# A third split of one inner product in five stages of a three-level Strassen kernel, with an operand half made earlier and a later place for additions

## The chip, the cores and the metric

The kernel runs on one core of a Trainium2 chip. The metric is the device time of one execution in microseconds (us). The kernel before takes 1354.5 us (median of 3 runs, 1354.32 to 1354.63).

## The reference

```python
probs = softmax(router_logits, axis=-1)               # 16 x 512 x 8
for e in range(8):
    expert_out = np.matmul(x, expert_weights[e])      # x: 16 x 512 x 512, weights: 512 x 2048
    output += probs[:, :, e:e+1] * expert_out         # output: 16 x 512 x 2048, float32
```

Read as one product, 8192 rows of z (the row of x times each of the eight probabilities, 4096 values) are multiplied with a 4096 x 2048 matrix.

## The kernel before, in words

**Three levels.** The product is taken apart by the Strassen-Winograd scheme. At the outer level there are seven products P1 to P7 (the dictionary key `r` in `products[r, q]`), each for 16 row pairs `q`; one operand of a product is 256 rows (`HQ`) by 1024 columns of z as two tiles `t[0]` and `t[1]` of 128 x 8 x 256 (f16), the other a set of weight tiles. At the inner level each product is again seven *steps*, in the order 1, 5, 6, 2, 7, 3, 4 (`STEPS`); a step is 8 matmuls of 128x128 by 128x512 into one PSUM bank of 512 f32 columns. The step's letter a or b below says which of a stage's two products it belongs to (5a is step 5 of the first). At the third level, where it is used, one step of *both* products of a stage (16 matmuls of 512 columns) is replaced by seven *small* products of 4 matmuls of 256 columns each. They are called small 1 to small 7 here.

**Stages.** `add` makes a list of stages, each of one or two products, and `run(stage)` writes out its instructions. The order is P1 (7 stages), P2 (8), P5 and P6 together (17), then P7 and P4 in turn (16: a P7 stage of two products, then the P4 stage of the same rows), then P3 (9). `k5`, `k7` and `k3` are the first stages of P5/P6, of P7/P4 and of P3. `hooks[(stage, slot)]`, filled with `at`, holds loads and sums that are begun before a given slot (step) of a stage.

**Where the third level is used before.** `by_thirds` splits steps 1 and 5 in most stages (all P4 stages from the second on among them), `by_twos` step 2 in four P1 stages. P7's stages have none. In `by_thirds` the small products go through banks x and q; small 1 is copied by ScalarE (ACT) to the left half of bank g, small 2 is added on it by TensorE (PE), and small 3's result is added by VectorE (DVE) into the right half of g. Bank h gets small 7 in its right half (DVE) and small 4 in its left half (ACT, line L931). In `by_thirds` small 2 comes before small 3.

**Order of the work.** PE, DMA and the vector work all keep the order in which they are written. For DVE that order comes from a planner: `later` queues a task with a cost in us, and `slack`, called after each step, moves a clock for PE forward by the slot's length and issues tasks while the clock for DVE is behind it:

```python
def slack(slot=SLOT, lag=LAG):
    clock["dve"] = max(clock["dve"], clock["pe"])
    clock["pe"] += slot
    while queue and clock["dve"] < clock["pe"] - lag:
        queue.popleft().run()
```

After it comes the step's `post`: the addition or copy that takes the step's result out of its bank. Where a product has a base (P6, P7, P4), `post` of steps 1, 5, 6, 7, 3 and 4 is a DVE addition of 128x512 f32 with a tile of 128 x 512 f32 (`half()`, from a pool `h` of 12 tiles), and `post(1)` writes a further bank b on which step 2 accumulates. `need(task)` flushes the queue to a task whose result a step reads.

**Tiles of P7 and P4.** The eight tiles of a P7 stage's results serve as the base of the P4 stage behind it, and are freed when that stage's transfers to the output (POOL's queue, `out_dram<-h`) have landed. The next P7 stage's eight bases are fetched into h tiles in between (SP's queue, `h<-out_dram`), at slots 7, 9, 12 and 16 of the P4 stage, counted on into the P7 stage. `Left.make(k)` makes an operand half with one multiplication and one subtraction, `queue_s2` and `queue_i` make the sums `s2` (pool d, 3 tiles) and `i` from it; `queue_halves` queues them for the next P7 stage in the P4 stage, half 0 at slot 5 and half 1 at slot 11. `Thirds.queue` queues a P4 stage's operands in the P7 stage ahead of it.

**P3.** `turnover_in_place` loads P3's weights during the last P7/P4 pair and makes their sums: tasks of 2.29 us, put at the head of the queue. `EARLY` lists operand halves of P3 that are made during P6 and kept in DRAM.

Of the kernel before, what the change touches and what calls it, by code (L numbers as in the profile page):

```python
# [31 lines left out]
def kernel(  # L32
# [7 lines left out]
    nc = tc.nc  # L40
    P = 128
# [13 lines left out]
    HQ = 256  # L55
# [17 lines left out]

    def x_tile():
        return xpool.tile([P, C, HQ], f16, name="xs", tag="x")

    def h_tile(shape, dtype):
        return hpool.tile(shape, dtype, name="h", tag="h")
# [276 lines left out]
    SLOT = 1.73  # L355
    STEPS = (1, 5, 6, 2, 7, 3, 4)
    HP = HQ // 2
    LAG = 0.3
# [89 lines left out]
    class Left:  # L448
# [34 lines left out]

        def queue_s2(self):
            def make():
                self.s2 = spool.tile([P, K8, HP], f16, name="d", tag="d")
# [50 lines left out]
        def half(self, k):  # L537
            return self.t[k]

    class HalfLoadedLeft(Left):  # L540


        def __init__(self, xb, pb, kept, source):
            super().__init__(xb, pb, kept=kept)
            self.source = source

        def load(self):
            self.t[0] = new_z()
            sp(self.t[0], self.source)

        def queue_make(self, k):
            if k == 0:
                self.task[0] = None
            else:
                super().queue_make(k)

# [13 lines left out]
    class Thirds:  # L570
# [14 lines left out]
            tt(o, *(self.s[v] if isinstance(v, int) else v for v in (x, y)), op)  # L585
            self.s[p] = o

        def queue(self):
            self.a.queue_make(0)
            self.b.queue_make(0)  # L590
            for p in (5, 6, 3, 7):
# [3 lines left out]
            for left in (self.a, self.b):  # L595
                left.queue_make(1)

        def op(self, p, part):
            need(self.task[7])
            a, b = self.a.t[0], self.b.t[0]  # L600
            z = {1: a[:, 0:C], 2: a[:, C:K8], 4: b[:, C:K8]}.get(p)
            return (self.s[p] if z is None else z)[:, :, ds(part * HP, HP)]

    class Right:

# [45 lines left out]
    class Product:  # L651
# [4 lines left out]
            self.loads, self.banks, self.o = [], {}, {}  # L656
            self.apart = self.two = False

        def step(self, p):
            b = "q" if p in (5, 3) else "b" if p == 2 else "x"  # L660
            if p in (1, 5):
                self.banks[b] = (bank if p == 1 else bank2)()
# [100 lines left out]
    def left_of(r, q, fresh=True):  # L763
        a, b = 2 * q, 2 * q + 1
        if r == 1:
            pt = PBlock(a, P1, xp1[q - 2][1] if q in (2, 3) else None)
            if q in (2, 3):
                xs[a] = XBlock(a, xp1[q - 2][0])
            return Left(xblock(a), pt), [xblock(a), pt]
        if r == 2:  # L770
            pt = PBlock(a, P2)
            return Left(xblock(a), pt), [xblock(a), pt]
        if r == 7:
            pt = PBlock(b, P2)
# [11 lines left out]
        if r == 3 and q in EARLY:  # L786
            pa = PBlock(a, P2)
            return HalfLoadedLeft(xblock(a), pa, ZHalf(q, z_places[q]), operand3[q]), [xblock(a), pa]
# [44 lines left out]
        return p  # L833

    products = {}
    EARLY = {5: (5, 3), 8: (8, 3), 10: (10, 9)}
    operand3 = {q: dram.tile([P, K8, HQ], f16, name=f"operand3_{q}") for q in EARLY}
    z_room = []

    def z_place(i):  # L840
        def place():
            if i != 2:
                z_room.append(new_w().rearrange("p k (two t) -> p (k two) t", two=2))
            return z_room[-1][:, ds(i // 2 * K8, K8), :]
        return place
    z_places = {q: z_place(i) for i, q in enumerate((5, 8, 10))}


    def start_loads(stage):
# [90 lines left out]
    def by_twos(stage):  # L940
# [36 lines left out]

        def full(i, p):
            some[i].step(p)
            slack()  # L980
            some[i].post(p)
        for slot, todo in enumerate((((1,), (0, 6)), ((5,), (6,)), ((1, 6),), ((2,), (7,), (3,)), ((0, 7),), ((4,), (1, 7))), 4):
            for make in hooks.get((stage, slot), ()):
# [6 lines left out]
                finish_loads(stage + 2)  # L990
        return 10

    def queue_lefts(stage):
        if stage in thirds:
            if not thirds[stage].task:
                thirds[stage].queue()
        elif stage < len(stages):
            for p in stages[stage]:
                queue_left(p.left)

    def run(stage):
        some = stages[stage]
        if stage in twos:
            twos[stage].queue()
        for p in some:
            p.left.queue_i()
        n = by_thirds(stage) if stage in thirds else 0
        if stage in twos:
            n = by_twos(stage)
        for i in range(n // 2, len(some[0].steps)):  # L1010
            for p in some:
                for make in hooks.get((stage, n), ()):
                    make()
                p.step(p.steps[i])
                slack()
# [36 lines left out]
        add(product(4, q), product(4, q + 1))  # L1052
    xs.clear()
    k3 = add(product(3, 5))
    for q in ((8, 10), (0, 14), (1, 2), (3, 4), (6, 7), (9, 11), (12, 13)):
        add(*(product(3, i) for i in q))
    end = add(product(3, 15))
    for stage in range(k7, k3, 2):
# [18 lines left out]
            at(*where, lambda q=q, tn=tn: joined(q, tn))  # L1077
    at(k6 - 1, 8, lambda: queue_left(lefts[7, 14]))

    def queue_halves(q, k):  # L1080
        for i in range(2):
            lefts[7, q + i].queue_make(k)
        if k == 0:
            for i in range(2):
                lefts[7, q + i].queue_s2()
    for n, q in enumerate(ORDER_7[1:], 1):
# [5 lines left out]
            for where, k in (((stage - 2, 12 + i), 0), ((stage - 1, 4), 1)):  # L1092
                at(*where, lambda q=q + i, k=k: lefts[7, q].onto.begin(k))
        for slot, k in ((5, 0), (11, 1)):
            at(stage - 1, slot, lambda q=q, k=k: queue_halves(q, k))

    def wedge(kn, e):

# [205 lines left out]
    def turnover_in_place(r, raw, loads, sums):  # L1304
# [35 lines left out]
    for stage, slot, q, k in ((k3 - 1, 2, 5, 0), (k3 - 1, 6, 5, 1), (k3 - 1, 7, 8, 0), (k3 - 1, 9, 10, 0),  # L1340
                              (k3 - 1, 10, 8, 1), (k3 - 1, 12, 10, 1)):
        left = lefts[3, q]
        at(stage, slot, left.load if k == 0 else left.kept.begin)
    at(k3, 0, load_z(0))
    early_p = {}

    def early_begin(q):
        early_p[q] = PBlock(2 * q, P2, h_tile([P, 2, HQ], f16))
        sp(early_p[q].t, p_dram[2 * q, ds(P2, 2), :].partition_broadcast(P))

    def early_make(q):
        of = lefts[6, q]
        flush(of.task[0])
        u = new_u()
        times(u, 0, of.xb, early_p[q])
        tt(u, u, of.t[0], SUB)
        sp(operand3[q], u)
    for q, (stage, slot) in EARLY.items():
        at(*slots_after(k5 + stage - 1, slot, 7), lambda q=q: early_begin(q))
        at(k5 + stage, slot, lambda q=q: later(2.45, lambda: early_make(q), True))  # L1360
    third2, third3 = {}, {}

    def third_at(stage, slot, of, r, p):
# [8 lines left out]
    third_at(ND, 5, third2, 2, 1)  # L1372
    third_at(ND, 7, third2, 2, 5)
    third_at(k3 - 2, 12, third3, 3, 1)
    third_at(k3 - 1, 6, third3, 3, 5)
    wait_for[k3 - 1] = 9
    wait_for[k3] = 1
    third4 = {}
# [20 lines left out]
            at(k7, 8 + 2 * i + j, lambda p=p, r=r: third_sum(p, r))  # L1399
    for p in (1, 5):  # L1400
        at(k7 + 1, 6, lambda p=p: third_sum(p, 7))


    def add_kept(q, n, t):
# [99 lines left out]
```

## Time and profile before

| | |
|---|---|
| median of 3 runs | 1354.5 us |
| the profiled execution | 1354.04 us, of which the span is 1352.3 us |
| PE busy | 1345.7 us, 7062 matmuls |
| DVE busy | 1153.5 us, 1446 instructions |
| ACT busy | 274.7 us |
| POOL busy | 404.5 us |
| granted PE clock | 0.9 or more of full speed in every slice, 1.00 over the span |

Busy PE time counts matmuls that overlap, so it says nothing of the rate at which they start; that is read from the starts of matmuls in the timeline. A P7 stage is 112 matmuls of 512 columns, a P4 stage from the second on 56 of 256 columns and 80 of 512.

### The profile page before, as it was taken

Reading aid. Unit: us, or ns where it says so; the run is one execution under the profiler, and the core shown is the slowest. Engines: PE = TensorE matmul, PEld = TensorE weight load, DVE = VectorE, ACT = ScalarE, POOL = GpSimd, SP = SyncE. Lnnn points to the kernel's source line nnn. Section 1 sums busy time; section 2 is a strip of 40 time slices with the busy share of each in tenths; the row PEclk is TensorE's granted clock in tenths of the full one; section 3 lists DMA queues with packets and bytes.
Section 4 is the critical chain, followed back from the end, with each engine's and each line's share of the span. In section 5 each row is a group of like instructions: output and inputs, shape, how many; then the busy total and the mean of one; then the engine's idle time right before and its main releaser. Section 6 shows DMA issues by size and latency. Waiting matters only on the chain.

```text
span 1352.3 us, 19284 instructions
## 1 busy us (share of the span) xinstructions
PE 1345.7 (100%) x7062; PEld 687.9 (51%) x7062; DVE 1153.5 (85%) x1446; ACT 274.7 (20%) x573; POOL 404.5 (30%) x619
## 2 busy tenths in 40 slices
PE   9999999999999999999999999999999999999998
PEld 4566655565544444444444444554555455556564
DVE  7878898888889889798887899888988988988886
ACT  3233423232211111111111100110111011224331
POOL 3223323333223332323312113424333221232342
PEclk9999999999999999999999999999999999999999
DMA  9999979999899999999988897999999989999997
GB/s 187 245 221 237 266 243 237 301 301 269 230 322 302 318 282 297 290 315 264 349 265 270 299 328 158 241 263 207 232 249 225 218 223 333 250 252 234 221 167 127
DMA packets 185391, 346.12 MB, mean 256 GB/s; under 512 B 52176, under 2 KB 81488, under 8 KB 181200
## 3 DMA queue, kind: packets, MB, share of 16 engines
q0 software_dynamic: 84960, 176.72, 57.5%
q1 hardware_dynamic: 97024, 146.02, 35.5%
q10 hardware_dynamic: 3312, 22.15, 4.5%
q8 instruction: 55, 0.90, 0.3%
q14 instruction: 40, 0.33, 0.1%
HBM read 203.59 MB, written 173.74 MB: 279 GB/s over the span
## 4 chain that ended last, share of the span: by engine, by line
PE 83%; issue 10%; POOL 3%; DMA 2%; DVE 1%; POOLq 0%; ACT 0%; DVEq 0%
PE ps L133 65%; PE pt L133 18%; POOL out_dram L124 2%; DMA w<-wd 1%; DMA wd<-w 1%; DVE h L110 1%; DMA out_dram<-h 1%; POOL wd L124 0%; DMA w<-in_x_dram 0%; DVE z L110 0%; POOL w L124 0%; POOL xs L124 0%; DVE w L110 0%; DVE ps L110 0%; POOLq L124 0%
## 5 line engine op out<-in xcount | busy, mean ns | idle before, releaser
L133 PE MATMUL ps<-w,z 128*128 128x512 f16 (+1 forms) x3784 | 818.3, 372 | 0.3 <-DVE z L110 0.3
L133 PEld LDWEIGHTS <-z 128*128 128x128 f16 x5256 | 514.1, 98 | 546.5 <-DVE z L110 0.8
L124 POOL DMA_DIRECT2D out_dram<-h x380 | 249.2, 663 | 729.7 <-ACT h L704 321.8
L133 PE MATMUL pt<-w,z 128*128 128x512 f16 (+1 forms) x1444 | 286.3, 343 | 0.0
L110 DVE TENSOR_TENSOR h<-ps,h 128x512 f32<-128x512 f32 x298 | 202.3, 687 | 81.5 <-PE ps L133 68.2
L110 DVE TENSOR_TENSOR z<-xT,pT 128x2048 f16<-128x2048 f16 x189 | 228.2, 1217 | 0.8 <-DMA xT<-xs 0.8
L133 PE MATMUL ps<-w,d 128*128 128x512 f16 x880 | 199.9, 379 | 0.6 <-DVE ps L110 0.6
L691 ACT COPY h<-ps 128x512 f32<-128x512 f32 x102 | 59.8, 586 | 393.9 <-PE ps L133 382.9
L133 PEld LDWEIGHTS <-d 128*128 128x128 f16 x880 | 86.1, 98 | 98.4 <-issue 1.2
L110 DVE TENSOR_TENSOR z<-z,d 128x2048 f16<-128x2048 f16 x110 | 132.0, 1217 | 0.0
L110 DVE TENSOR_TENSOR w<-w 128x1024 f16<-128x1024 f16 (+2 forms) x102 | 115.2, 1145 | 3.2 <-DMA w<-wd 2.4
L110 DVE TENSOR_TENSOR h<-pt,h 128x512 f32<-128x512 f32 x95 | 64.9, 687 | 32.4 <-PE pt L133 30.3
L704 ACT COPY h<-ps 128x512 f32<-128x512 f32 x54 | 31.6, 586 | 289.8 <-PE ps L133 247.2
L110 DVE TENSOR_TENSOR d<-z 128x1024 f16<-128x1024 f16 x110 | 73.5, 685 | 0.7
L110 DVE TENSOR_TENSOR ps<-ps,h 128x256 f32<-128x256 f32 (+1 forms) x84 | 50.5, 603 | 21.4 <-PE ps L133 16.8
L687 ACT COPY h<-ps 128x512 f32<-128x512 f32 x89 | 49.9, 599 | 69.8 <-PE ps L133 67.0
L124 POOL DMA_DIRECT2D kept<-h x56 | 30.7, 549 | 87.7 <-DVE h L110 47.2
L110 DVE TENSOR_TENSOR z<-z 128x2048 f16<-128x2048 f16 (+1 forms) x52 | 50.5, 978 | 1.6
L683 ACT COPY ps<-ps 128x512 f32<-128x512 f32 x47 | 26.8, 570 | 107.9 <-PE ps L133 71.6
L110 DVE TENSOR_TENSOR h<-h 128x512 f32<-128x512 f32 (+2 forms) x69 | 45.1, 675 | 0.1
L124 POOL DMA_DIRECT2D out_dram<-kept x40 | 41.1, 1134 | 0.3 <-issue 0.2
L133 PEld LDWEIGHTS <-h 128*128 128x128 f16 x384 | 37.5, 98 | 4.4
(99 smaller groups left out, 645.2 us busy)
## 6 DMA issues: line engine op xcount, KB each, us to landing
out_dram<-h POOLq DMA_DIRECT2D x380, 256.0 KB, 7.0
z<-z SPq DMA_DIRECT2D x56, 512.0 KB, 8.1
pT<-p_dram SPq DMA_DIRECT2D x94, 256.0 KB, 7.5
h<-kept SPq DMA_DIRECT2D x88, 256.0 KB, 7.4
w<-wd ACTq DMA_DIRECT2D x20, 1024.0 KB, 9.0
w<-in_expert_weights_dram POOLq DMA_DIRECT2D x33, 512.0 KB, 11.3
xT<-x SPq DMA_DIRECT2D x64, 256.0 KB, 6.5
h<-out_dram SPq DMA_DIRECT2D x60, 256.0 KB, 8.1
```

Source lines behind the costliest of these rows:

```text
L110: dve(nc.vector.tensor_tensor(out=o, in0=a, in1=b, op=op))
L124: note(nc.gpsimd.dma_start(out=o, in_=i, **how))
L133: note(nc.tensor.matmul(ps, z, w, start=start, stop=stop, skip_group_check=True))
L683: act(nc.scalar.copy(self.banks["b"], x))
L687: act(nc.scalar.copy(o[tn], q if p == 5 else x))
L691: act(nc.scalar.copy(o[TN[p]], b if p == 2 else x))
L704: act(nc.scalar.copy(o[tn], b))
```

## The change

1. In five P7 stages (`ONES = k7 + 6`, every second stage up to `k3`) step 1 of both products becomes seven small products (`by_ones`), put between full steps in the order: small 1, small 5, 5a, small 6, small 3, small 2, small 7, 5b, small 4, 6a, 2a, 6b, 2b; then 7, 3 and 4 as before. Their left operands are four DVE instructions per stage (`Ones.make`), their right operands four sums made once (`ones_sum`). The small products use the two banks x and q; step 5 of both products goes to banks of the other pool. Small 3's addition into the right half of bank g is written ahead of small 2's matmuls, which go into the left half of g; `post(1)` of the first product comes behind small 2. ACT's copies of small 5 and small 6 go into a fresh h tile, `keep`.
2. `slack` gets a third way to decide (`late`): issue tasks while DVE's clock plus the task's cost is below PE's clock plus 2.6 (1.6 in `by_twos`). It is used in slots 4 to 11 of all stages with two products, and for the full steps but step 5 in `by_ones`. Tasks are then issued ahead of a step's `post` more often, and the additions stand later in DVE's order.
3. The second operand half of P3's row pair 5 is made in P6's stage `k5 + 6` and loaded at `k3 - 1`, instead of being made in P3's first stage.
4. In the P7 stages the P4 operand halves are all queued ahead of the third-level sums (`whole_first`).
5. P3's row pairs are paired in another order, so that pair 14 comes two stages later; two sums of P3's weights are queued at slot 8 of stage `k3 - 1` instead of slot 3, one at 11 instead of 10, and the third-level sums of P3's step 5 at slot 9 instead of 6.

```diff
-    def slack(slot=SLOT, lag=LAG):
+    def slack(slot=SLOT, lag=LAG, late=None):
         clock["dve"] = max(clock["dve"], clock["pe"])
         clock["pe"] += slot
-        while queue and clock["dve"] < clock["pe"] - lag:
+        while queue and clock["dve"] < (clock["pe"] - lag if late is None else clock["pe"] + late - queue[0].cost):
             queue.popleft().run()
...
+    def by_ones(stage):
+        some, of = stages[stage], ones_[stage]
+        c0, c1 = (ds(i * HQ, HQ) for i in range(2))
+        x, q = bank2(), bank2()
+        g, qa = bank(), bank()
+        h, qb = bank(), bank()
+        some[0].banks["x"], some[1].banks["x"] = g, h
+        keep = half()
+
+        def small(r):
+            o = q[:, c1] if r in (5, 3) else g[:, c0] if r == 2 else x[:, c0]
+            z, w = of.op(r), of.weights[r]
+            for c in range(C):
+                mm(o, z[:, c, :], w[:, c, :], r in (1, 5) and c == 0, c == C - 1)
+            slack(0.4375, 1.3)
+            if r == 1:
+                act(nc.scalar.copy(g[:, c0], x[:, c0]))
+            elif r == 5:
+                act(nc.scalar.copy(keep[:, c1], q[:, c1]))
+            elif r == 6:
+                act(nc.scalar.copy(keep[:, c0], x[:, c0]))
+            elif r == 7:
+                evacuated(0.42)
+                tt(h[:, c1], x[:, c0], keep[:, c1], ADD)
+            elif r == 3:
+                evacuated(0.42)
+                tt(g[:, c1], q[:, c1], keep[:, c0], ADD)
+            elif r == 2:
+                some[0].post(1)
+            elif r == 4:
+                act(nc.scalar.copy(h[:, c0], x[:, c0]))
+                some[1].post(1)
+
+        def full(i, p):
+            some[i].step(p, (qa, qb)[i])
+            slack(late=LATE if p != 5 else None)
+            some[i].post(p)
+        for slot, todo in enumerate((((1,), (5,)), ((0, 5),), ((6,), (3,), (2,), (7,)), ((1, 5),),
+                                     ((4,), (0, 6)), ((0, 2),), ((1, 6),), ((1, 2),))):
...
+                (small if len(what) == 1 else full)(*what)
+        return 8
...
                 p.step(p.steps[i])
-                slack()
+                slack(late=LATE if len(some) == 2 and 4 <= n < 12 else None)
                 p.post(p.steps[i])
...
-    for q in ((8, 10), (0, 14), (1, 2), (3, 4), (6, 7), (9, 11), (12, 13)):
+    for q in ((8, 10), (0, 1), (2, 3), (4, 14), (6, 7), (9, 11), (12, 13)):
...
-                      ((7, (k3 - 1, 3)), (5, (k3 - 1, 3)), (6, (k3 - 1, 10)), (4, (k3, 3))))
+                      ((7, (k3 - 1, 8)), (5, (k3 - 1, 8)), (6, (k3 - 1, 11)), (4, (k3, 3))))
...
-    third_at(k3 - 1, 6, third3, 3, 5)
+    third_at(k3 - 1, 9, third3, 3, 5)
```

More of the change, by code (lines that the diff above doesn't have):

```diff
@@ L75, in x_tile, with d_tile @@
         return xpool.tile([P, C, HQ], f16, name="xs", tag="x")
+    def d_tile():
+        return spool.tile([P, K8, HP], f16, name="d", tag="d")
     def h_tile(shape, dtype):
@@ L485, in make @@
             def make():
-                self.s2 = spool.tile([P, K8, HP], f16, name="d", tag="d")
+                self.s2 = d_tile()
                 tt(self.s2, self.t[0][:, :, ds(HP, HP)], self.t[0][:, :, ds(0, HP)], SUB)
@@ L586, in make, with queue @@
             self.s[p] = o
-        def queue(self):
+        def queue(self, whole_first=False):
             self.a.queue_make(0)
             self.b.queue_make(0)
+            if whole_first:
+                self.a.queue_make(1)
+                self.b.queue_make(1)
             for p in (5, 6, 3, 7):
@@ L594, in queue @@
                 left.queue_s2()
-            for left in (self.a, self.b):
-                left.queue_make(1)
+            if not whole_first:
+                self.a.queue_make(1)
+                self.b.queue_make(1)
         def op(self, p, part):
@@ L602, in op, with __init__, make, queue @@
             return (self.s[p] if z is None else z)[:, :, ds(part * HP, HP)]
+    class Ones:
+        def __init__(self, a, b, weights):
+            self.a, self.b, self.weights, self.s, self.task = a, b, weights, {}, {}
+        def make(self, p):
+            e0, e1, rows = ds(0, C), ds(C, C), ds(0, HP)
+            a, b = self.a.t[0], self.b.t[0]
+            if p in (5, 3):
+                self.place = x_tile().rearrange("p c (two t) -> p two c t", two=2)
+            x, y, op = {5: (b[:, e0, rows], b[:, e1, rows], ADD), 6: (5, a[:, e0, rows], SUB),
+                        3: (a[:, e1, rows], 6, SUB), 7: (a[:, e0, rows], b[:, e0, rows], SUB)}[p]
+            o = self.place[:, 0 if p in (5, 3) else 1]
+            tt(o, *(self.s[v] if isinstance(v, int) else v for v in (x, y)), op)
+            self.s[p] = o
+        def queue(self):
+            for p in (5, 6, 3, 7):
+                self.task[p] = later(0.42, lambda p=p: self.make(p))
+        def op(self, r):
+            need(self.task[7])
+            if r in self.s:
+                return self.s[r]
+            left, e = {1: (self.a, 0), 2: (self.a, C), 4: (self.b, C)}[r]
+            return left.t[0][:, ds(e, C), ds(0, HP)]
     class Right:
@@ L785, in left_of @@
             return Left(xblock(a), pt, of=lefts[5, q]), [xblock(a), pt]
-        if r == 3 and q in EARLY:
+        if r == 3 and (q, 0) in EARLY:
+            sources = {k: operand3[q, k] for k in range(2) if (q, k) in EARLY}
+            if len(sources) == 2:
+                return LoadedLeft(None, None, None, sources), []
             pa = PBlock(a, P2)
-            return HalfLoadedLeft(xblock(a), pa, ZHalf(q, z_places[q]), operand3[q]), [xblock(a), pa]
+            return LoadedLeft(xblock(a), pa, ZHalf(q, z_places[q]), sources), [xblock(a), pa]
         if r == 3 and q < KEPT_Z:
@@ L835 @@
     products = {}
-    EARLY = {5: (5, 3), 8: (8, 3), 10: (10, 9)}
-    operand3 = {q: dram.tile([P, K8, HQ], f16, name=f"operand3_{q}") for q in EARLY}
+    EARLY = {(5, 0): (5, 3), (5, 1): (6, 3), (8, 0): (8, 3), (10, 0): (10, 9)}
+    operand3 = {what: dram.tile([P, K8, HQ], f16, name="operand3") for what in EARLY}
     z_room = []
@@ L979, in full @@
             some[i].step(p)
-            slack()
+            slack(late=LATE_TWOS)
             some[i].post(p)
@@ L991, in by_twos @@
         return 10
+    ones_ = {}
+    def by_ones(stage):
[35 more added lines that the diff above has]
+                                     ((4,), (0, 6)), ((0, 2),), ((1, 6),), ((1, 2),))):
+            for make in hooks.get((stage, slot), ()):
+                make()
+            if slot == 1:
+                queue_lefts(stage + 1)
+            if slot == 5:
+                store_loads(stage + 1)
+            if slot == 7:
+                finish_loads(stage + 2)
+            for what in todo:
+                (small if len(what) == 1 else full)(*what)
+        return 8
     def queue_lefts(stage):
@@ L995, in queue_lefts @@
             if not thirds[stage].task:
-                thirds[stage].queue()
+                thirds[stage].queue(k7 <= stage < k3)
         elif stage < len(stages):
@@ L1006, in run @@
             p.left.queue_i()
-        n = by_thirds(stage) if stage in thirds else 0
+        n = by_thirds(stage) if stage in thirds else by_ones(stage) if stage in ones_ else 0
         if stage in twos:
@@ L1078, with queue_halves @@
     at(k6 - 1, 8, lambda: queue_left(lefts[7, 14]))
-    def queue_halves(q, k):
+    def queue_halves(q, k, stage):
         for i in range(2):
@@ L1083, in queue_halves @@
         if k == 0:
+            if stage in ones_:
+                ones_[stage].queue()
             for i in range(2):
@@ L1094 @@
         for slot, k in ((5, 0), (11, 1)):
-            at(stage - 1, slot, lambda q=q, k=k: queue_halves(q, k))
+            at(stage - 1, slot, lambda q=q, k=k, stage=stage: queue_halves(q, k, stage))
     def wedge(kn, e):
@@ L1339, in load_z, with early_begin, early_make @@
         return load.begin
-    for stage, slot, q, k in ((k3 - 1, 2, 5, 0), (k3 - 1, 6, 5, 1), (k3 - 1, 7, 8, 0), (k3 - 1, 9, 10, 0),
+    for stage, slot, q, k in ((k3 - 1, 2, 5, 0), (k3 - 1, 5, 5, 1), (k3 - 1, 7, 8, 0), (k3 - 1, 9, 10, 0),
                               (k3 - 1, 10, 8, 1), (k3 - 1, 12, 10, 1)):
         left = lefts[3, q]
-        at(stage, slot, left.load if k == 0 else left.kept.begin)
+        at(stage, slot, (lambda k=k, left=left: left.load(k)) if (q, k) in EARLY else left.kept.begin)
     at(k3, 0, load_z(0))
+    at(k3, 3, load_z(1))
     early_p = {}
[L1347 to L1351, printed above, removed]
+    def early_begin(what):
+        q, k = what
+        early_p[what] = PBlock(2 * q, P2, h_tile([P, 2, HQ], f16))
+        sp(early_p[what].t, p_dram[2 * q, ds(P2 + 2 * k, 2), :].partition_broadcast(P))
+    def early_make(what):
+        q, k = what
         of = lefts[6, q]
-        flush(of.task[0])
+        flush(of.task[k])
         u = new_u()
[L1355 to L1360, printed above, removed]
+        times(u, 0, of.xb, early_p[what])
+        tt(u, u, of.t[k], SUB)
+        sp(operand3[what], u)
+    for what, (stage, slot) in EARLY.items():
+        at(*slots_after(k5 + stage - 1, slot, 7), lambda what=what: early_begin(what))
+        at(k5 + stage, slot, lambda what=what: later(2.45, lambda: early_make(what), True))
     third2, third3 = {}, {}
@@ L1401, with ones_sum, make @@
         at(k7 + 1, 6, lambda p=p: third_sum(p, 7))
+    ones7 = {}
+    def ones_sum(r):
+        def make():
+            w = right[7].w[1].rearrange("p (k c) (h n) -> p k c h n", k=2, h=2)
+            b = {kn: w[:, kn[0], :, kn[1]] for kn in BLOCKS}
+            if r == 5:
+                ones7.update({1: b[0, 0], 2: b[1, 0], 3: b[1, 1], 7: b[0, 1]})
+            if r != 7:
+                ones7[r] = d_tile().rearrange("p (c two) t -> p c (two t)", two=2) if r == 4 else x_tile()
+            x, y = {5: (7, 1), 6: (3, 5), 4: (2, 6), 7: (3, 7)}[r]
+            tt(ones7[r], ones7[x], ones7[y], SUB)
+        later(0.69, make)
+    ONES = k7 + 6
+    for r, where in zip((5, 6, 4, 7), ((ONES - 4, 9), (ONES - 4, 10), (ONES - 2, 9), (ONES - 2, 10))):
+        at(*where, lambda r=r: ones_sum(r))
+    for stage in range(ONES, k3, 2):
+        ones_[stage] = Ones(*(p.left for p in stages[stage]), ones7)
     def add_kept(q, n, t):
```

29 lines of the change are left out of this document (14 added, 15 removed).

## The prediction

> **What bounds the kernel now.** I read the page, then what PE waited for, then the timeline around those places and through one P7/P4 pair.
>
> ```profile
> span 1352.3 us, 19284 instructions
> PEclk9999999999999999999999999999999999999999
> PE ps L133 <- DVE ps L110: 0.6, 2, 0.4
> PE ps L133 <- DVE z L110: 0.3, 1, 0.3
> 1178.83 17.27 PE ps L133 x80
> ```
>
> The clock is full, and behind the start PE waited three times in all, each time for DVE. The last line (the chain) has 80 matmuls of 512 columns in 17.27 us: 0.2159 us each, 1.727 a step. Between the waits PE streams, so only two things move the time: columns taken out of PE's stream, and waits put in or taken away. The three waits in the timeline:
>
> ```profile
> 418.05 0.81 PE L133 MATMUL pt<-w,z 128*128 128x512 f16 x3
> 419.25 0.59 PE L133 MATMUL ps<-w,d 128*128 128x512 f16 x2 [0.39 <-DVE ps L110]
> 769.12 0.81 PE L133 MATMUL pt<-w,z 128*128 128x512 f16 x3
> 770.14 0.59 PE L133 MATMUL ps<-w,d 128*128 128x512 f16 x2 [0.22 <-DVE ps L110]
> 1149.20 2.32 PE L133 MATMUL ps<-w,z 128*128 128x512 f16 x10
> 1145.43 4.61 DVE L110 TENSOR_TENSOR w<-w 128x4096 f16<-128x4096 f16 x2
> 1150.55 1.22 DVE L110 TENSOR_TENSOR z<-z,d 128x2048 f16<-128x2048 f16 x1
> 1151.83 2.33 PE L133 MATMUL ps<-w,z 128*128 128x512 f16 x10 [0.31 <-DVE z L110]
> ```
>
> Starts against the cadence: 418.05 + 3 x 0.2159 = 418.70, next start 419.25, lost 0.55 us; likewise 0.37 and 0.47 us. The third is in the last P4 stage: two weight sums of P3 (4.61 us) stood ahead of the sum `i` that step 7b reads. PE went on 0.06 us after that sum's end (1150.55 + 1.22).
>
> **Columns.** How the small products run is seen in a P4 stage that has them:
>
> ```profile
> 946.40 1.04 PE L133 MATMUL pt<-w,z 128*128 128x256 f16 x8
> 946.60 0.69 DVE L110 TENSOR_TENSOR h<-ps,h 128x512 f32<-128x512 f32 x1 [1.03 <-PE ps L133]
> 949.46 1.04 PE L133 MATMUL pt<-w,xs 128*128 128x256 f16 x8
> 950.16 0.86 DVE L110 TENSOR_TENSOR ps<-pt,h 128x256 f32<-128x256 f32 x2 [0.60 <-PE pt L133]
> 950.33 0.60 PE L133 MATMUL ps<-w,xs 128*128 128x256 f16 x4
> 950.76 0.60 PE L133 MATMUL pt<-w,z 128*128 128x256 f16 x4
> 950.97 2.55 DVE L110 TENSOR_TENSOR ps<-ps,h 128x256 f32<-128x256 f32 x4
> 952.51 3.40 PE L133 MATMUL ps<-w,d 128*128 128x512 f16 x15
> ```
>
> From 946.40 to 952.51 stand 56 matmuls of 256 columns: 0.1091 us each, 0.436 a small product. A split takes out 16 x 0.2159 = 3.454 and puts in 28 x 0.1091 = 3.055: 0.40 us less, in five stages **-2.0 us**. The Trainium skill, "TensorE: Matmul & The Clock Gate", section "Back-to-back issue gap", gives a sustained 81 ns at 128 columns and 131 ns at 512. My estimate from that page, on a straight line by columns, is 98 ns at 256, so 2.10 us taken out for 2.74 put in, and a split would lose 0.6 us. The rows above decide against it: 0.2159 and 0.1091.
>
> **The wait that the change adds.** In `by_ones` small 3's addition into the right half of bank g is written ahead of small 2's matmuls into the left half. Is a bank ordered as a whole, or by halves? The trace has the nearest case: ACT's copy of small 4 (L931) goes into the left half of h, whose right half DVE wrote with small 7's result. The copy reads nothing of DVE's.
>
> ```profile
> ACT ps L931 <- DVE ps L110: 19.3, 14, 1.8
> L931 ACTq EVENT_SEMAPHORE  x17: 17/17/17, 256.3 to 1141.6; - x17
> ```
>
> Yet it waits for DVE in all 14 cases of the P4 stages, and has a waiting instruction of its own for it. I conclude that another engine's write into the other half is waited for. The Trainium skill, "PSUM — Partial Sum Buffer", section "PSUM bank collisions raise a hardware error", has the rule that speaks against this order: guard PSUM by bank and quadrant, not by address. By that rule PE waits in every one of the five stages; by addresses it would not, which is the rival of halves ordered apart.
>
> How long? Counted from the P7 stage's start: small 1 to 0.44, small 5 to 0.87, 5a to 2.60, small 6 to 3.04, small 3 to 3.47, where small 2 is due. DVE's order comes from the planner's own clock; I added its costs slot by slot over a pair of stages. At the P4 stage's last slot DVE's clock is 0.01 us behind PE's, under the 0.3 that it needs, so one operand task (multiplication and subtraction, half 1 of P7's second product) lands behind the addition of 4b and ahead of that of 5a. Before, the same task runs here:
>
> ```profile
> 967.80 1.28 DVE L110 TENSOR_TENSOR h<-ps,h 128x512 f32<-128x512 f32 x2
> 969.00 1.22 DVE L110 TENSOR_TENSOR u<-xT,pT 128x2048 f16<-128x2048 f16 x1
> 970.25 1.22 DVE L110 TENSOR_TENSOR z<-u,z 128x2048 f16<-128x2048 f16 x1
> 971.39 0.68 DVE L110 TENSOR_TENSOR h<-ps,h 128x512 f32<-128x512 f32 x1
> 971.99 0.69 DVE L110 TENSOR_TENSOR ps<-ps,h 128x512 f32<-128x512 f32 x1
> ```
>
> So the addition of 4b starts at 0.20 (946.60 after 946.40) and the task at 0.80; 971.39 - 969.00 = 2.39 later, at 3.19, that of 5a; 0.60 later, at 3.79, small 3's, which takes 0.43 (0.86 for two). PE goes on 0.06 behind it, at 4.28: **0.81 us of waiting a stage, +4.05 us in five**. Were DVE free, small 3's addition would start 0.21 after its matmuls (950.97 against 950.76) and PE would lose 0.70; that is the lower end, +3.5. Small 4 comes 1.73 after small 7, whose addition ends 0.8 after it: no wait. Likewise 7b, the tightest return to a bank (6b, then 2b, 7a): by the same count 6b's addition ends 1.1 us before 7b is due.
>
> **The fresh tile.** ACT copies small 5 into `keep`, then small 6; small 3's addition reads that. `keep` is claimed when all 12 h tiles are in use: the P4 stage's eight and four fetched bases; 2a's and 2b's go to the next two bases, so `keep` gets 7a's, once its transfer has landed. Before, the next base fetch took that tile:
>
> ```profile
> SPq L121 <- DMA out_dram<-h: 303.0, 65, 21.9
> 914.78 0.86 POOL L124 DMA_DIRECT2D out_dram<-h  x1 [0.87 <-DVE h L110]
> 926.26 0.33 SPq L121 DMA_DIRECT2D h<-out_dram  x1
> 962.33 0.86 POOL L124 DMA_DIRECT2D out_dram<-h  x1 [0.97 <-DVE h L110]
> 968.79 0.33 SPq L121 DMA_DIRECT2D h<-out_dram  x1
> out_dram<-h POOLq DMA_DIRECT2D x380, 256.0 KB, 7.0
> ```
>
> A P7 stage starts at 952.51 + 17.27 = 969.78, the one before at 922.23: 946.40 less 112 matmuls of 0.2159 us. So the tile was free 1.0 us before the stage in one case and 4.0 us after it in the other, the first of the five. Later additions put 7a's issue up to 1.4 us later. The tile has to be there by about 2.9 us (two ACT copies of 0.37 and hand-overs ahead of 3.79):
>
> ```profile
> L919 ACT COPY h<-pt 128x256 f32<-128x256 f32 x28 | 10.4, 372 | 1.8
> L110 DVE TENSOR_TENSOR z<-z 128x512 f16<-128x512 f16 x16 | 6.4, 422 | 0.3
> 922.23:946.40 24.17, 24.17 (x114) 10.97 (x112) 19.82 (x26) 1.17 (x2) 9.03 (x13) 1.00 1.04 241
> 946.40:969.78 23.38, 23.38 (x138) 13.29 (x137) 20.66 (x27) 4.09 (x10) 8.50 (x12) 1.00 1.08 253
> ```
>
> With a tile at 4.0 to 5.4 one stage loses 1.1 to 2.5 more; none if that landing (11.5 us against a median of 7.0) does not recur. I take one such stage, **+1.7 us**; the other end is 0, or all five.
>
> **What costs nothing while its cover holds.** DVE: four instructions of 0.42 and two of 0.43 a stage, 2.55 us. A pair has 47.55 - 19.82 - 20.66 = 7.1 us of DVE idle (the two rows above, fourth group); cover gone, it is 2.55 a pair. ACT: four copies of 0.37 beside 1.17 us busy. The weight sums (four, once) and P3's half made in P6 (2.4 us, taken off P3's first stage) lie in DVE's idle as well; its store and load replace the loads of x, p and half a z on SP's queue. The two x tiles that the sums hold make the next pair's x and p loads wait for P4's operands; `whole_first` brings these forward. Later additions: a post may now end 3.3 us behind its step (2.6 + 0.69), and in ordinary stages PE comes back to that bank after three steps, 5.18 us.
>
> **Waits that go.** The 0.47 us in the last P4 stage goes: at slot 8 the sum `i` is done before the weight sums are queued, and these end some 2.7 us before 4a needs the bank. **-0.47 us.** Late next is the step behind 7a there. The waits at 418 and 769 us stay: they fall in stages of one product, where the new rule doesn't hold, and by the planner's clock the same tasks stand ahead of the addition.
>
> **Sum.** -2.0 + 4.05 - 0.47 + 1.7 = +3.3. The profiled execution (1354.04: span 1352.3 and 1.7 around it) would be 1357.3; it is 0.46 under the median of 1354.5, on which I forecast **1357.8 us**, 1356.6 to 1359.0 in this case.
>
> **Rivals.**
>
> No late tile: all as above without the 1.7, 1356.1 us. For it: four of the five landings before came in time by the case at 962.33. Chance 0.31.
>
> Halves are ordered apart, so small 2 doesn't wait: -2.0 - 0.47, 1352.0; if the later additions also free the two other waits, 1351.1. For it: only that no PE matmul in this trace stands behind a DVE write to the other half; against it, L931. Chance 0.12, half of it beyond 1351.8. This is also the case in which the change does what it says.
>
> Landings are late in most of the five stages: the DMA share stands at 1.04 and 1.08 in the two rows above, and every further landing over 2.9 us after the stage's start costs its excess. With 1.7 in all five: 1354.5 + 1.58 + 8.5 = 1364.6. Against it: the 962.33 case has 3.9 us to spare. Chance 0.12.
>
> The later additions take PE: from the point where DVE runs over 1.9 us behind its plan (5.18 - 3.3), each such step costs its excess; two or three stages with 1 us each give 1360. Against: DVE's idle above. Chance 0.07.
>
> **How the numbers follow.** The forecast's case has 0.38. About 0.2%, 2.7 us, is what a measurement of this kernel can tell from no change: below 1351.8 or above 1357.2. Slower: 0.30 of the forecast's 0.38, 0.12, 0.07: 0.49. Faster: 0.06. The rest, 0.45, lies within. The range 1352.0 to 1361.0 leaves out the faster tail (0.06) and most of the late landings (0.10).
>
> **What would show it.** Five PE waits for `DVE ps` of about 0.8 us, each behind small 3, some 3.5 us into a P7 stage; one longer, with ACT's first copy into h waiting for an output transfer just ahead; the wait at 1151 us gone, those at 418 and 769 still there; 60 matmuls more (5 x 12). I am wrong if small 2 follows small 3 without a gap, or if PE waits in many stages outside these five.

## The result, and the profile after

The changed kernel takes 1357.55 us (median of 22 runs, 1356.38 to 1367.37), the kernel before 1354.36 us on the same chip (22 runs, 1353.73 to 1355.06): a ratio of 1.0029 [1.0019, 1.0039]. A ratio is one of means, and most kernels with the later additions have single executions 6 to 10 us over their median, which stand in it; medians are named beside it for that reason.

The profiled execution took 1356.46 us, 2.42 more than before's. The page's head and PE's waits of the kernel after (lines of the code stand three further down than before):

```profile
span 1354.8 us, 19477 instructions
PE 1344.0 (99%) x7122; PEld 693.7 (51%) x7122; DVE 1166.8 (86%) x1480; ACT 281.6 (21%) x593; POOL 403.9 (30%) x619
PE ps L136 <- DVE ps L113: 3.4, 6, 0.6
PE pt L136 <- ACT h L1052: 1.0, 1, 1.0
```

Sixty matmuls more, as five splits make. Behind the start, PE's waits for DVE's work on banks (`ps`) rose from two to six, the one for `z` is gone, and a new one for ACT's copy into `keep` (L1052) stands beside them. The second of the split stages, PE's timeline and then DVE's:

```profile
973.72 0.60 PE L136 MATMUL pt<-xs 128*128 128x256 f16 x4
974.15 0.60 PE L136 MATMUL pt<-w,xs 128*128 128x256 f16 x4
975.39 0.60 PE L136 MATMUL ps<-w,z 128*128 128x256 f16 x4 [0.64 <-DVE ps L113]
971.92 1.21 DVE L113 TENSOR_TENSOR u<-xT,pT 128x2048 f16<-128x2048 f16 x1
973.17 1.23 DVE L113 TENSOR_TENSOR z<-u,z 128x2048 f16<-128x2048 f16 x1
974.32 0.68 DVE L113 TENSOR_TENSOR h<-ps,h 128x512 f32<-128x512 f32 x1
974.92 0.42 DVE L113 TENSOR_TENSOR ps<-pt,h 128x256 f32<-128x256 f32 x1
```

Small 3 ends its turn at 974.15 + 0.44 = 974.59; small 2, due there, starts at 975.39. In between stand the operand task, 5a's addition and then small 3's, as forecast. From the starts of matmuls, small 2 lost 0.801, 0.801, 0.801 and 0.803 us in the last four split stages, and 0.755 in the first. That first stage, on POOL, ACT and PE:

```profile
916.13 0.86 POOL L127 DMA_DIRECT2D out_dram<-h  x1 [2.44 <-DVE h L113]
925.82 0.37 ACT L1052 COPY h<-pt 128x256 f32<-128x256 f32 x1 [2.75 <-DMA out_dram<-h]
924.62 0.60 PE L136 MATMUL pt<-xs 128*128 128x256 f16 x4
926.25 0.60 PE L136 MATMUL pt<-w,xs 128*128 128x256 f16 x4 [1.03 <-ACT h L1052]
927.43 0.60 PE L136 MATMUL ps<-w,z 128*128 128x256 f16 x4 [0.59 <-DVE ps L113]
```

The output transfer of 7a's tile, issued at 916.13, holds ACT's copy until 925.82. Small 3 writes the half of bank q that this copy reads, so PE waits there already (1.19 us), not at small 2 only. Last, the end of the last P4 stage, DVE and then PE:

```profile
1149.51 1.21 DVE L113 TENSOR_TENSOR z<-z,d 128x2048 f16<-128x2048 f16 x1
1150.64 0.68 DVE L113 TENSOR_TENSOR h<-ps,h 128x512 f32<-128x512 f32 x1
1151.24 4.61 DVE L113 TENSOR_TENSOR w<-w 128x4096 f16<-128x4096 f16 x2
1149.12 7.07 PE L136 MATMUL ps<-w,z 128*128 128x512 f16 x32
```

The weight sums (4.61) now stand behind the sum `i`, and PE streams. Stage by stage against the trace before, the starts shift by +0.34 (start-up), -0.55 (the wait at 419, gone), +1.54 (the first split stage), four times +0.40 and -0.48 (the last P4 stage): +2.45, the whole difference of the spans.

### The profile page after: what moved, and what is told of

The parts are those of the page before. It is cut to its first block, busy times and chain, and to the rows that moved or that the text cites. A ratio compares the mean times of both kernels' runs of the same rounds, so it can differ in the third digit from the quotient of the medians.

```text
span 1354.8 us, 19477 instructions
## 1 busy us (share of the span) xinstructions
PE 1344.0 (99%) x7122; PEld 693.7 (51%) x7122; DVE 1166.8 (86%) x1480; ACT 281.6 (21%) x593; POOL 403.9 (30%) x619
## 5 line engine op out<-in xcount | busy, mean ns | idle before, releaser
L136 PE MATMUL ps<-w,z 128*128 128x512 f16 (+1 forms) x3884 | 840.0, 372 | 3.1 <-DVE ps L113 3.1
L113 DVE TENSOR_TENSOR h<-ps,h 128x512 f32<-128x512 f32 x318 | 214.6, 684 | 62.1 <-PE ps L136 60.1
L136 PE MATMUL pt<-w,z 128*128 128x512 f16 (+1 forms) x1304 | 253.2, 338 | 0.0
L113 DVE TENSOR_TENSOR h<-pt,h 128x512 f32<-128x512 f32 x75 | 51.0, 685 | 27.1 <-PE pt L136 22.9
```

The source lines that it names most:

```text
L113: dve(nc.vector.tensor_tensor(out=o, in0=a, in1=b, op=op))
L136: note(nc.tensor.matmul(ps, z, w, start=start, stop=stop, skip_group_check=True))
```

## The experiments

The theory was that two waits, small 2 for small 3's addition and one late `keep`, use up what the columns save. Its rivals: the waits cost nothing beside something else (the later additions, the early half), or the split itself brings nothing.

**1. The addition behind small 2's matmuls.**

```diff
-            elif r == 3:
+            elif r == 2:
                 evacuated(0.42)
                 tt(g[:, c1], q[:, c1], keep[:, c0], ADD)
-            elif r == 2:
                 some[0].post(1)
```

> Only the writing order changes: small 3's addition into the right half of g is written behind small 2's matmuls; PE's own order (6, 3, 2, 7) and every instruction stay. Theory (a PSUM bank is ordered as a whole, and PE waits for the addition): the five waits of 0.80 us ahead of small 2 go, -4.0 us against the changed kernel, so about 1353.5 us; what ACT's late tile costs at small 3 stays. Rival (the waits come from VectorE being late with small 3's operand or from elsewhere, not from the bank's other half): no change, 1357.5 us.

Measured: median 1353.12 us (before on that chip 1354.53; ratio 1.0001 [0.9988, 1.0015]). PE in the same stage:

```profile
973.26 0.60 PE L136 MATMUL pt<-xs 128*128 128x256 f16 x4
973.70 0.60 PE L136 MATMUL pt<-w,xs 128*128 128x256 f16 x4
974.14 0.60 PE L136 MATMUL ps<-w,z 128*128 128x256 f16 x4
```

Small 2 follows small 3 after 0.44. The five waits are gone with one instruction put behind four matmuls, and the median is 4.4 us below that of the change. The wait at small 3 stays (1.22 us). That the waits cost nothing is refuted. Bank g is one tile in the program, so no run tells whether it is the bank or the tile that is ordered as a whole.

**2. `keep` claimed sooner.** In `by_ones`, `keep = half()` became `keep = ones_keep[stage]`, and:

```diff
+        at(stage - 1, 11, lambda stage=stage: ones_keep.__setitem__(stage, half()))
```

> Only the claim of keep moves: ahead of the fetches of the last four bases, at slot 11 of the P4 stage, so that it gets 2a's tile and not 7a's. Theory (the wait at small 3 in the first split stage is ACT's wait for 7a's transfer): that wait goes, -1.1 us in a profile like the changed kernel's, -1 to -2.2 in the median (1355.3 to 1356.5), and the five waits of 0.80 stay; the fourth base fetched (the second product's quarter for step 6) comes about 2 us later, which may delay 6b's addition. Rival (the transfers as a whole are late, whatever tile is claimed): PE waits as long somewhere else, 1357.5 us.

Measured: 1356.99 us, ratio 1.0024 [1.0012, 1.0036]. The edit didn't do what it says; ACT's waits and the next base fetch on SP's queue show it:

```profile
ACT h L1052 <- DMA out_dram<-h: 2.5, 1, 2.5
```

```profile
917.28 0.33 SPq L124 DMA_DIRECT2D h<-out_dram  x1
```

The copy still waits for 7a's transfer, and the fetch still gets 2a's tile: where the name is claimed did not decide which tile it gets. That its first use decides fits this, but no other run tests it. Nothing follows for the theory.

**3. Both edits.**

> Both edits: the addition behind small 2 and keep claimed early. Theory: the sum of the two, -5 to -6.2 us, 1351.3 to 1352.5 us: faster than the kernel before by what the columns save (2.0) and by the two waits that the change removed (0.47 and 0.55). Rival: the two waits hide one another, so that the second edit brings nothing once the first is made, 1353.5 us.

Measured: 1353.48 us, ratio 1.0001 [0.9989, 1.0013], a miss for the reason just told: its profile has a wait of 1.67 us at small 3.

**4. `keep` in a tile of another pool.**

```diff
-        keep = half()
+        keep = zpool.tile([P, 2, NB], f32, name="z", tag="z")[:, 0]
```

> Only keep's place changes: a tile of the operand pool z, of which four are free when a split stage starts, in place of an h tile. Theory: ACT's copy of small 5 no longer waits for the transfer of 7a's result, so the wait at small 3 in the first split stage goes and that at small 2 stays 0.80 there too: -1.2 us in a profile, -1 to -2.2 in the median, 1355.3 to 1356.5 us. Rival (transfers are late as a whole): the same time as the changed kernel, 1357.5, with PE's wait at another place.

Measured: 1356.17 us, ratio 1.0021 [1.0009, 1.0033]. The wait at small 3 is gone, small 2 waits 0.80 in all five stages: the h tile was worth 1.4 us in the medians (1357.55 - 1356.17, on two chips whose medians of the kernel before differ by 0.10).

**5. Edits 1 and 4 together** (version 5 below).

> keep in a z tile and small 3's addition written behind small 2. Theory: no PE wait in the five stages at all; 1353.1 of the run with the addition moved alone, less 1.2 to 1.6 for the late tile: 1351.5 to 1352.0 us. Against the kernel before that is -2.0 for the columns and -1.0 for the two waits that went. Rival: a further wait is late next (the fetched bases, which get 7a's and 7b's tiles), 1353 us.

Measured: 1351.92 us, ratio 0.9988 [0.9976, 0.9999]: 5.6 us below the change and faster than the kernel before. In its trace every split stage takes 23.777 us against 24.173 without a split: 0.397 us less, 1.98 in five.

**6. No split at all**, the rest of the change kept.

```diff
-    ONES = k7 + 6
+    ONES = k3
```

with the list of `ones_sum` places empty.

> The changed kernel without the split: step 1 of the five stages in full again, and no sums for it; the later additions, the early half of P3, and the moved sums stay. Theory: 2.0 us of columns come back and all waits inside the five stages go; against the kernel before only the two removed waits remain, -1.0 us, about 1353.4 us. Rival (the later additions or the moved P3 work cost time of their own, hidden behind the split's waits): at or above the kernel before, 1354.4 us or more.

Measured: 1353.95 us, ratio 1.0005 [0.9992, 1.0018]. The theory had 1353.4 and its rival 1354.4 or more; the median lies between. Against version 5 it is 2.03 more, or 1.76 with each taken against the kernel before on its own chip: about the columns once again. Its profile caught a long execution (1361.96 us), DVE first, then PE:

```profile
540.75 1.23 DVE L113 TENSOR_TENSOR u<-xT,h 128x2048 f16<-128x2048 f16 x1 [6.69 <-DMA h<-p_dram]
543.75 0.69 DVE L113 TENSOR_TENSOR d<-z 128x1024 f16<-128x1024 f16 x1
544.35 0.69 DVE L113 TENSOR_TENSOR h<-ps,h 128x512 f32<-128x512 f32 x1
545.09 5.29 PE L136 MATMUL ps<-w,z 128*128 128x512 f16 x16 [4.51 <-DVE h L113]
```

DVE stood 6.69 us at the load for P3's added early half; the addition of 6a is behind it in DVE's order, and PE waits for that at 7a. Its 8 us over the median are three waits of PE in P6 (0.54, 1.36 and 4.67 us from the starts of matmuls), behind a late base, a late load for an early half that the kernel before makes too, and this one, and 1.7 us at a lower clock behind the last.

**7. Without P3's second early half**, on version 5: `(5, 1)` is left out of `EARLY`, and the half is made in P3's first stage.

> As the run before it (addition behind, keep in z), and the second operand half of P3's pair 5 is made in P3's first stage again. Theory: the executions that are 8 to 10 us longer come from VectorE waiting in P6 for the early half's probabilities, so none of them here; the median as in the run before it, or up to 0.5 us more if P3's first stage now waits. Rival (they come from the later additions): as many long executions as there.

Measured: 1355.69 us, ratio 1.0006 [0.9997, 1.0014]: 3.8 more than version 5. DVE and PE in P3's first stage:

```profile
1159.42 1.22 DVE L113 TENSOR_TENSOR z<-xT,pT 128x2048 f16<-128x2048 f16 x1
1160.67 1.23 DVE L113 TENSOR_TENSOR z<-z,w 128x2048 f16<-128x2048 f16 x1
1161.81 4.82 DVE L113 TENSOR_TENSOR w<-w 128x1024 f16<-128x1024 f16 x5
1166.54 1.22 DVE L113 TENSOR_TENSOR z<-z,d 128x2048 f16<-128x2048 f16 x1
1167.82 3.18 PE L136 MATMUL ps<-w,z 128*128 128x512 f16 x8 [2.14 <-DVE z L113]
```

The half is made again (first two lines), and the sum for 7a comes 2.3 us too late for PE; 1.7 us at a lower clock follow. The expectation allowed 0.5 us for this. No execution lies above 1357.36, as it expected; experiment 12 says what that is worth.

**8. The old rule in `slack` everywhere**, on the change as it is.

```diff
-        while queue and clock["dve"] < (clock["pe"] - lag if late is None else clock["pe"] + late - queue[0].cost):
+        while queue and clock["dve"] < clock["pe"] - lag:
```

> The changed kernel with the planner's old rule everywhere (no later additions). Theory: the five waits at small 2 stay (0.70 to 0.81 each), the wait of 0.55 us in P6's first stage is back, and 7a's transfer starts up to 1.4 us earlier, so the late tile costs less: 1356.5 to 1358 us. Rival (the later additions are needed to have VectorE's work done in the split stages): more waits in the five stages, 1360 us or more.

Measured: 1364.2 us, ratio 1.0073 [1.0061, 1.0085], a miss of 6 us and more. The split's waits stay, 0.75 to 0.88 at small 2 and 1.30 at small 3 in the first stage, so the later additions are not what makes the tile late. The 0.55 at 419 us, expected back, is not there. In the last P4 stage 7b now waits 4.5 us:

```profile
1152.58 1.22 DVE L113 TENSOR_TENSOR z<-z,d 128x2048 f16<-128x2048 f16 x1
1153.71 4.61 DVE L113 TENSOR_TENSOR w<-w 128x4096 f16<-128x4096 f16 x2
1158.84 1.22 DVE L113 TENSOR_TENSOR z<-z,d 128x2048 f16<-128x2048 f16 x1
1160.11 10.23 PE L136 MATMUL ps<-w,z 128*128 128x512 f16 x34 [4.36 <-DVE z L113]
```

With additions in their old place, the weight sums moved to slot 8 come between the two sums `i`.

**9. The weight sums back in their old slots**, on version 5, with the later rule: slots 3, 3 and 10 for 8, 8 and 11, and 6 for 9.

> The fastest version with the two weight sums of P3 at slot 3 of the last P4 stage again, as in the kernel before. Theory: the wait of 0.47 us ahead of 7b there is back, 0.4 to 0.5 us. Rival (the later additions alone removed it): no wait there.

Measured once: 1354.11 us; PE loses 2.20 us at 7a of the last P4 stage, where the kernel before lost 0.47 at 7b. Rule and places belong together: each without the other costs more there than having neither.

**10. P4's operand tasks ahead of 4b's and 4a's additions**, on the change: the later rule up to slot 13 in the stages ahead of a split one.

> The changed kernel with the new planner rule in the last two slots of the P4 stages ahead of split stages too, so that the operand task stands ahead of 4b's addition. Theory (PE's wait at small 2 is the chain of VectorE's work behind 4b): VectorE is free when small 3 ends, and the wait falls from 0.80 to 0.70 us, its floor (0.21 to start, 0.43, 0.06). Rival (the wait is set by ACT's copies or the hand-over between engines): 0.80 as before.

Measured once: 1361.04 us, a long execution. Small 2 loses 0.757 in each of the five stages, not 0.70: with DVE free, that is the floor of this hand-over, and all that stood ahead of it in DVE's order cost 0.05 a stage. Where the execution got long, DVE and PE:

```profile
488.55 0.69 DVE L113 TENSOR_TENSOR h<-h 128x512 f32<-128x512 f32 x1 [3.80 <-DMA h<-kept]
492.16 0.68 DVE L113 TENSOR_TENSOR h<-ps,h 128x512 f32<-128x512 f32 x1
492.89 5.30 PE L136 MATMUL ps<-w,z 128*128 128x512 f16 x16 [2.56 <-DVE h L113]
```

Here it is a base, not the early half's load, that lands late; the addition that PE needs is again behind the task that waits.

**11. The early half's load seven slots sooner**, on version 5.

> The fastest version so far (addition behind small 2, keep in z), with the probabilities for the added early half of P3 loaded seven slots (12 us) sooner. Theory (the executions of 1360 us and more come from VectorE waiting in P6 for this load, which lands 0.02 us before its use in the traces where the three others have 5 to 11 us): none of them in some 11 runs, median 1351.9 as without the edit. Rival (they come from transfers that are late for other reasons): one or two of them again.

Measured: 1352.38 us (1351.59 to 1356.33), ratio 0.999 [0.9981, 0.9999]. None is near 1360, as the theory had it, but the highest two of 11, 1356.33 and 1355.58, are still 3 to 4 us over the median.

**12. The later rule from the first P7 stage on only**, on version 5.

```diff
-                slack(late=LATE if len(some) == 2 and 4 <= n < 12 else None)
+                slack(late=LATE if len(some) == 2 and 4 <= n < 12 and stage >= k7 else None)
```

> As the version with small 3's addition behind small 2 and keep in a z tile (median 1351.92 us, lowest 1351.62, one of 11 executions 1361.59), but with the later additions only from the first P7 stage on; P1, P2, P5 and P6 keep the old rule. Theory: in P6 the later additions bring nothing but the 0.55 us wait at 419 us, and they put tasks that read late loads (the joined sums, P3's early halves) ahead of the addition of 6a, for which PE then waits at 7a by 2 to 5 us in the executions that exceed the median by 5 to 13 us. So the 0.55 may come back (median 1351.9 to 1352.6) and no execution lies above 1358. Rival: the late loads alone make PE wait, in either order of DVE; then executions of 1360 and more remain, as often as 1 in 8. A third: the old rule changes which tasks are left for P2 to P6's later stages, and a new wait of over 1 us stands there (median above 1353).

Measured: 1352.18 us (1351.50 to 1353.27), ratio 0.9983 [0.9974, 0.9992]: the lowest ratio of all, though its interval overlaps those of versions 5 and 11; there is no long execution. Above 1359 us lay 11 of the 113 timed executions of the change and the eight versions that keep the later rule in P6 (1 to 7 and 11), none of 116 of the kernel before. At that rate 11 without one would come by luck 1 time in 3. At the place of the second trace (a base landing late) this version keeps the same order on DVE; at that of the first, the addition of 6a still stands behind the task that waits for the early half's load, and only 1.2 us nearer to it than in version 5 (2.41 us from the task's start to the addition's, against 3.61). Versions 7 and 11, which keep the later rule in P6 but not that load, or load it sooner, have none in 22 either; at the rate of the other seven, 11 in 91, luck would give that 1 time in 17. So the cause is not settled, and the added load is as much a suspect as the rule. Shown twice is the mechanism: a late load, a DVE task waiting for it, an addition behind that task, PE behind that addition. That the later rule in P6 makes it likelier is argued only.

This version also bears on the wait at 419 us; see below.

## Why the prediction was right

Forecast 1357.8, measured 1357.55; the sum of its terms +3.3, measured +3.2 in the medians. That the two are so close is partly luck. In the profiled pair the change is +2.45: the fresh tile cost 0.6 less than its term, and -0.55 at 419 us and +0.34 at the start were not in the sum. The remaining 0.7 lies between the profiled executions and the medians, and no run divides it into terms.

**Columns** (-2.0): 0.397 a stage, 1.98 in five, and 1.8 to 2.0 by experiments 5 and 6. The row of small products in the P4 stages was the right price. **Small 2's wait** (5 x 0.81): 0.80 in four stages, 0.755 in one; experiment 1 gives the cause. The conclusion from L931, that another engine's write into the other half of a bank is waited for, held, and the rival of halves ordered apart falls. The Trainium skill's rule for PSUM ("PSUM — Partial Sum Buffer", section "PSUM bank collisions raise a hardware error") agrees with these five waits. The lower end of 0.70 was too low, by 0.05: small 3's addition started 0.26 behind its matmuls and PE 0.06 behind its end.

**The fresh tile** (+1.7): 1.19 at small 3 less 0.05 at small 2 in the profile, 1.4 by experiment 4. Right in cause and stage; the size came out near the lower end, 1.1. The transfer was issued 1.35 us later than before (916.13 against 914.78), as forecast, but held the tile 9.7 us and not 11.5. In the six traces with an h tile the wait at small 3 came each time in the first split stage alone, 0.96 to 1.67 us long. The step that failed is the place: the text let the late tile act through small 3's addition, and didn't see that small 3's own matmuls overwrite what the copy has yet to read. **The wait in the last P4 stage** (-0.47): -0.48. **769 us**: stays, 0.378 against 0.37.

**The wait at 418 us** was said to stay and is gone: -0.55. The step that failed is the reason, "by the planner's clock the same tasks stand ahead of the addition". In the trace before, DVE had lost 2.4 us some 30 us earlier:

```profile
386.06 2.29 DVE L110 TENSOR_TENSOR w<-w 128x4096 f16<-128x4096 f16 x1 [1.00 <-DMA w<-wd]
391.00 2.29 DVE L110 TENSOR_TENSOR w<-w 128x4096 f16<-128x4096 f16 x1 [1.44 <-DMA w<-wd]
```

In version 12, which has the old rule there, DVE and PE show:

```profile
417.43 1.23 DVE L113 TENSOR_TENSOR z<-z 128x2048 f16<-128x2048 f16 x1
418.57 0.69 DVE L113 TENSOR_TENSOR ps<-ps,h 128x512 f32<-128x512 f32 x1
419.81 1.89 PE L136 MATMUL ps<-w,d 128*128 128x512 f16 x8
```

The same tasks stand ahead of the addition, yet DVE met no late landing, PE had started 1.1 us later into the kernel, and nothing waits. Version 8, with the old rule everywhere, has no wait there either. So that wait belonged to one execution's landings as much as to an order, and whether the median of the kernel before contains it is open. The change as it is puts that task ahead of 4a's addition, which would have ended the wait too: the new rule in a stage of two products reached over into the stage of one behind it.

**Covers.** DVE's additions cost PE nothing: 13.3 us more busy, and in version 5 no wait of over 0.38 us behind the start-up. Two prices were wrong without harm to the sum. P3's early half was costed at nothing; taken out, it costs 3.8 us (experiment 7). Its trace has 4.82 us of weight sums between the half and the sum for 7a; that the third-level sums moved to slot 9 are what took the room there is argued from this order, and no run moves them back alone. And the tail of long executions was in no term; the rival of the later additions came nearest, but looked to DVE's work and not to landings. The tail moves means, not medians.

## What to carry to other kernels

Before a new addition is written ahead of matmuls, look whether they go into the same PSUM bank, in whichever half: moving one instruction behind four matmuls turned 0.3% lost here, together with a scratch tile from another pool, into 0.1% gained. A tile that is claimed when its pool is full inherits the landing of somebody else's transfer; choose the pool by what its last user waits for. And a wait read in one trace may have its cause tens of us earlier in a landing: before counting on it, follow the waiting engine's own waits back.

## What the runs showed of the hardware

After a wait of some length PE came back at half its cadence. In the rows of the windows just behind the wait, for experiments 8, 6, 10, 7 and 9 in that order, the last three columns are the granted clock, the DMA share and GB/s:

```profile
1160.10:1165.00 4.90, 4.89 (x12) 1.75 (x13) 3.75 (x6) 0.00 (x0) 0.27 (x1) 0.50 0.91 201
```

```profile
545.10:549.00 3.90, 3.90 (x11) 1.43 (x11) 3.83 (x4) 0.00 (x0) 0.00 (x0) 0.56 0.99 325
```

```profile
492.90:496.90 4.00, 4.00 (x11) 1.50 (x11) 3.59 (x4) 0.00 (x0) 0.00 (x0) 0.57 1.06 379
```

```profile
1167.90:1171.60 3.70, 3.70 (x10) 1.31 (x11) 2.34 (x4) 0.00 (x0) 0.00 (x0) 0.55 1.07 346
```

```profile
1150.20:1154.00 3.80, 3.80 (x18) 1.77 (x19) 1.91 (x3) 0.00 (x0) 0.86 (x1) 1.00 1.07 314
```

Behind waits of 4.52, 4.67, 2.72 and 2.30 us the clock was 0.50 to 0.57, and 13, 8, 8 and 8 matmuls started some 0.21 us late each: 2.7 us on top of the first wait, 1.7 on the others. Behind one of 2.20 us, and behind all shorter ones in the kept traces, it stayed at 1.00. So neither the drop nor its price follows from the length of the wait: the longest, 4.67 us, cost less on top than that of 4.52.

The place in time matters too. In experiment 7 PE came back at 1167.82, and the clock fell only after that:

```profile
1164.90:1168.25 3.35, 1.21 (x6) 0.38 (x5) 3.35 (x3) 0.59 (x1) 0.86 (x1) 1.00 1.11 270
1168.30:1171.65 3.35, 3.35 (x10) 1.14 (x8) 1.99 (x4) 0.00 (x0) 0.00 (x0) 0.50 1.06 354
```

In the traces' record of the granted clock the stretches at half rate last 3.41 us in experiments 6, 7 and 10 and 6.83 in experiment 8, once and twice the same length, and the stretches at full rate are whole multiples of it as well (1163.94 us, 341 times, ahead of the drop in experiment 7). So the clock changed on a grid of 3.41 us that does not start with the wait. Counted on it, the wait of 2.30 us lies within one step (1164.87 to 1168.28), while that of 2.20 us is divided at 1148.66 into 0.66 and 1.54. That the idle share of one step decides fits all these waits, but no run moves a wait along the grid, so it is not shown.

The Trainium skill ("TensorE: Matmul & The Clock Gate", section "What's actually happening") tells of two rates, half and full, with half after an idle window of about 3.4 us whose phase is free. The half rate, the length and the free phase agree with the traces. An idle window, if it means one without any work, does not: 2.30 us of waiting within a step of 3.41 was enough in experiment 7.
